# Hybrid decoder layer with a product-key expert mixer: picks of the gathered block paced over all groups, three one-hot groups in ten from ScalarE, up rows three deep, gathers four turns later

## The chip, the cores and the metric

The kernel runs on one core of a Trainium2 chip. Time is device time of one execution in microseconds (us); the number to predict is the median of the runs of the changed kernel. Engines are named as in the profile: PE (TensorE), with PEld for its weight loads, DVE (VectorE), ACT (ScalarE), POOL (GpSimd) and SP (SyncE, which issues most DMAs).

## What is computed

One decoder layer on 512 tokens of width 1024. Its front half (gated DeltaNet heads, pooling groups, output projection) is not touched. The second half is a mixer over 128 x 128 = 16,384 single-neuron experts: for each token and each of 8 heads, 16 experts are found by product keys, and their outputs are added with a softmax gate.

```python
def block(xb):
    q = (xb @ w_query).reshape(t, PEER_HEADS, 2, PEER_HALF)
    scores = jnp.einsum("thpc,hpkc->thpk", q, sk)
    s1, i1 = lax.top_k(scores[:, :, 0], PEER_TOPK)
    s2, i2 = lax.top_k(scores[:, :, 1], PEER_TOPK)
    ...
    top_s, top_pos = lax.top_k(cand, PEER_TOPK)
    idx = jnp.take_along_axis(cand_idx, top_pos, axis=-1)
    gate = jax.nn.softmax(top_s, axis=-1)
    u = expert_down[idx]
    v = expert_up[idx]
    act = jax.nn.gelu(jnp.einsum("td,thkd->thk", xb, u), approximate=False)
    return jnp.einsum("thk,thkd->td", gate * act, v)
```

## The kernel before

The 512 tokens are four blocks of 128. Block 0 is the **gathered** block: its experts' rows are fetched by indirect DMA, one row tile (128 tokens x 1024) for each of its 128 slots, first from `down` and then from `up`. Blocks 1 to 3 (384 tokens) are **dense**: PE computes the hidden value of every expert (128 tiles of 128 experts, "tile" below), multiplies it by a gate matrix that is zero almost everywhere, and multiplies the product by `up`.

After the queries (`query`, `topk`) and the first 17 tiles (`make_ahead`), the second half of the program has three stages.

**The hole before the gates.** PE turns the dense blocks' indices and gates into rows by three groups of transposes, `i1a`, `i2a` and `ex` (the softmax's result). `ex` needs an exponential on ACT and four DVE instructions, and DVE copies the results to `i1t`, `i2t`, `gtt`.

**The gates.** 96 groups of four tokens. For a group DVE builds two one-hot factors: `ob` (position of the second key times the gate, four TENSOR_SCALAR, L850) and `oa` (position of the first key, one TENSOR_TENSOR, L852). PE multiplies them (`g_ps`, L857), ACT copies the result into `stg` (L860), POOL copies part of each full `stg` to `gsb` and SP writes the rest to DRAM (`gmat`). When the group's number mod 10 is in `A_ACT`, DVE makes only `ob` (one TENSOR_TENSOR, L841), and ACT makes `oa` from eight ACTIVATEs (L845, L846). `oa` and `ob` have four buffers each, `g_ps` six, `stg` one.

Between the groups two other things run. `take` spends **steps** of tiles on PE: a step is three matmuls (L126 to L128) and eight steps are a tile. Each tile needs its weights split into `w_hi` on ACT (L616) and `w_lo` on POOL (L617). And `picks` walks through the top-k of the gathered block on DVE in 28 pieces, which end in the indices `eidx` (L809) and the gates `gat`. A scheduler sets the order on each engine from the program order, priorities and modelled times; `issue_after` ties an instruction behind another in that order.

**The turns.** 128 turns of the last loop, one for each tile of experts. A turn loads a row block of `up` (`u_raw`, two buffers), splits it into `u_hi` (ACT) and `u_lo` (DVE, L121), multiplies hidden values and gates (`w`, DVE L957), splits that into `whi` and `wlo`, and PE adds 18 matmuls to `acc` (L940). Every fourth turn loads a new `gsb`. Most turns also compute one more tile (`refill`), with `w_lo` on DVE. The gathers run beside this: POOL issues a row (L915), DVE multiplies and adds it (L917), with four row buffers; `gather_goal` says how many of the 256 have been taken by the end of a turn. After the loop the outputs are normalised and written.

Of the kernel before, what the change touches and what calls it, by code (L numbers as in the profile page):

```python
# [7 lines left out]
F32 = mybir.dt.float32  # L8
# [10 lines left out]
P = 128  # L19
T = 512  # L20
D = 1024
DC = D // P
# [7 lines left out]
NK = 128  # L30
# [10 lines left out]
FAR = 26  # L41
S_QUERY = 7
S_WAIT = 10
S_FIRST = 16
AHEAD = RUN + FAR
LEAD = 4
FAR_TILES = [RUN + ((2 * k + 1) * (NK - RUN)) // (2 * FAR) for k in range(FAR)]
A_ACT = (2, 7)

C_ID, C_U, C_M0, C_MS, C_IO, C_ONE = 0, 128, 256, 384, 384 + 7 * 128, 384 + 8 * 128  # L50
C_RAT = 384 + 9 * 128
# [21 lines left out]
def hymba_peer_block(ctx, tc, consts, x, nmix, w_in, w_ba, conv_w, a_log, dt_bias, dn_w, w_pool, pool_scale,  # L73
                     w_out, nffn, w_q, sub_k, downT, down, up, nfin, out):
    nc = tc.nc
# [8 lines left out]
    iota = cst[:, C_IO:C_IO + P]  # L84
# [64 lines left out]
    with ExitStack() as fx:  # L149
# [227 lines left out]
        with ExitStack() as f2:  # L377
# [77 lines left out]
            steps = [(lv, tb) for lv in range(1, 7) for tb in range(NTB)]  # L455
# [201 lines left out]
    def ahead_steps():  # L657
        pair = load_pair(downT[ahead[made[0]]], nc.gpsimd)
        while made[0] < AHEAD:
            i, now = ahead[made[0]], pair  # L660
            made[0] += 1
            for k, _ in enumerate(s_steps(i, now)):
                if not k and made[0] < AHEAD:
                    pair = load_pair(downT[ahead[made[0]]], nc.gpsimd)
                yield
# [62 lines left out]
    def softmax(pool, dst, sc, behind=None):  # L728
        n = sc.shape[1]
        nc.vector.tensor_sub(dst, sc, sc[:, :, 0:1].broadcast_to([P, n, K]))  # L730
        with tc.issue_after(behind.ins) if behind is not None else ExitStack():
            nc.scalar.activation(dst, dst, AF.Exp)
        sm = pool.tile([P, n], F32, name="sm", bufs=1)
        nc.vector.tensor_reduce(sm, dst, axis=AX.X, op=ALU.add)
        nc.vector.reciprocal(sm, sm)
        nc.vector.tensor_tensor(dst, dst, sm[:, :, None].broadcast_to([P, n, K]), op=ALU.mult)

    with ExitStack() as fy:
        tk = fy.enter_context(tc.tile_pool(name="tk", bufs=2))
        p_pj = fy.enter_context(tc.tile_pool(name="p_pj2", bufs=2, space=PSUM))  # L740
        p_sc = fy.enter_context(tc.tile_pool(name="p_sc", bufs=4, space=PSUM))
        skt = tk.tile([P, 16, NK], F32, name="skt", bufs=1)
        nc.scalar.dma_start(out=skt, in_=sub_k)
        SA = [P, NDT, PH, K]
        i1a = tk.tile(SA, F32, name="i1a", bufs=1)
        i2a = tk.tile(SA, F32, name="i2a", bufs=1)
        tsa = tk.tile(SA, F32, name="tsa", bufs=1)

        def query(h, eng):
            qh = tk.tile([P, 2, T], F32, name="qh")  # L750
            w = [load_pair(w_q[2 * h + p], eng) for p in range(2)]
            ps = [p_pj.tile([P, 512], F32, name="q_ps") for p in range(2)]
            parts = [slice(0, T)] if h else [slice(0, T // 2), slice(T // 2, T)]
            for ts in parts:
                for p in range(2):
                    for c in range(DC):
                        mm3(ps[p][:, ts], (w[p][0][:, c, :], w[p][1][:, c, :]), (xn_hi[:, c, ts], xn_lo[:, c, ts]),
                            c == 0, c == DC - 1)
            for p in range(2):
                cp = nc.scalar.copy(qh[:, p], ps[p])  # L760
            behind[:] = [None, cp.ins]
            sc = tk.tile([P, NDT, 2, NK], F32, name="sc")
            ps = [p_sc.tile([P, 512], F32, name="sc_ps") for _ in range(NTB)]
            for p in range(2):
                for tb in range(NTB):
                    nc.tensor.matmul(ps[tb][:, p * NK:(p + 1) * NK], qh[:, p, tb * P:(tb + 1) * P],
                                     skt[:, 2 * h + p, :], start=(p == 0), stop=(p == 1))
            for tb in range(NTB):
                nc.scalar.copy(sc0[:, tb, h] if tb < NG else sc[:, tb - NG],
                               ps[tb][:, :2 * NK].rearrange("p (a k) -> p a k", a=2))  # L770
            return sc

        sc = query(0, nc.vector)
        for h in range(PH):
            sc_next = query(h + 1, nc.gpsimd) if h + 1 < PH else None
            for _ in topk(tk, sc, NDT, tsa[:, :, h, :], i1a[:, :, h, :], i2a[:, :, h, :]):
                pass
            sc = sc_next
            if sc is not None:
                make_ahead(h + 1)  # L780
        make_ahead(S_QUERY + S_WAIT)
        ex = tk.tile(SA, F32, name="ex", bufs=1)
        softmax(tk, ex.rearrange("p b h k -> p (b h) k"), tsa.rearrange("p b h k -> p (b h) k"), s_act[0])
        for src, dst in ((i1a, i1t), (i2a, i2t), (ex, gtt)):
            ps = p_pj.tile([P, 512], F32, name="q_ps")
            with tc.issue_after(s_last[0].ins):
                for b in range(NDT):
                    pe_last = nc.tensor.transpose(ps[:, b * P:(b + 1) * P], src[:, b].rearrange("p h k -> p (h k)"),
                                                  ident)
            nc.vector.tensor_copy(dst, ps[:, :TD])  # L790
            if dst is not i2t:
                nc.scalar.activation(n1t if dst is i1t else ngt, ps[:, :TD], AF.Copy, scale=-1.0)
# [3 lines left out]
    with ExitStack() as fy:  # L796
# [17 lines left out]
        gs = fy.enter_context(tc.tile_pool(name="gs", bufs=3))  # L814
        p_g = fy.enter_context(tc.tile_pool(name="p_g", bufs=6, space=PSUM))
        gsb0 = gp.tile([P, NTG, GN * TG], F32, name="gsb")

        steps = ahead_steps()
        taken = 0

        def take(goal):
            nonlocal taken, pe_last
            while taken < goal:
                with tc.issue_after(pe_last.ins):
                    next(steps, None)
                pe_last = s_last[0]
                taken += 1

        n_steps = (AHEAD - S_QUERY - S_WAIT) * DC
        take(S_FIRST)  # L830
        ng = 0
        for tg in range(NTG):
            stg = gs.tile([P, NK, TG], F32, name="stg", bufs=1)
            for q in range(TG // 4):
                oa = gs.tile([P, 4, P], F32, name="oa", bufs=4)
                ob = gs.tile([P, 4, P], F32, name="ob", bufs=4)
                ps = p_g.tile([P, 512], F32, name="g_ps")
                t0 = tg * TG + q * 4
                q4 = [P, 4, P]
                if ng % 10 in A_ACT:  # L840
                    nc.vector.tensor_tensor(ob, iota[:, None, :].broadcast_to(q4),  # L841
                                            i2t[:, t0:t0 + 4, None].broadcast_to(q4), op=ALU.is_equal)
                    for u in range(4):
                        t = t0 + u
                        nc.scalar.activation(oa[:, u], iota, AF.Abs, bias=n1t[:, t:t + 1])  # L845
                        nc.scalar.activation(oa[:, u], oa[:, u], AF.Relu, scale=ngt[:, t:t + 1], bias=gtt[:, t:t + 1])  # L846
                else:
                    for u in range(4):
                        t = t0 + u
                        nc.vector.tensor_scalar(ob[:, u], iota, i2t[:, t:t + 1], gtt[:, t:t + 1], op0=ALU.is_equal,  # L850
                                                op1=ALU.mult)
                    nc.vector.tensor_tensor(oa, iota[:, None, :].broadcast_to(q4),  # L852
                                            i1t[:, t0:t0 + 4, None].broadcast_to(q4), op=ALU.is_equal)
                ng += 1
                with tc.issue_after(pe_last.ins):
                    for u in range(4):
                        pe_last = nc.tensor.matmul(ps[:, u * P:(u + 1) * P], ob[:, u], oa[:, u], start=(u == 0),  # L857
                                                   stop=(u == 3))
                take(S_FIRST + ng * (n_steps - S_FIRST) // (TD // 4))
                nc.scalar.copy(stg[:, :, q * 4:q * 4 + 4], ps.rearrange("p (t i) -> p i t", i=NK))  # L860
                if ng * n_picks // (TD // 4) > picked:
                    next(picks)
                    picked += 1
            sv = stg.rearrange("p i t -> p (i t)")
            nc.gpsimd.tensor_copy(gsb0[:, tg, :], sv[:, :GN * TG])
            nc.sync.dma_start(out=gmat[tg, :, GN * TG:], in_=sv[:, GN * TG:])
# [4 lines left out]
    with ExitStack() as fz:  # L871
# [73 lines left out]
        for i in range(NK):  # L945
            if i and i % GN == 0:
                gsb = gp.tile([P, NTG, GN * TG], F32, name="gsb")
                nc.sync.dma_start(out=gsb, in_=gmat[:, :, i * TG:(i + GN) * TG].rearrange("g p x -> p g x"))
            raw = up_p.tile([P, D], F32, name="u_raw")
            nc.sync.dma_start(out=raw, in_=up[i * NK:(i + 1) * NK, :])  # L950
            uhi = up_p.tile([P, D], F32R, name="u_hi")
            ulo = up_p.tile([P, D], F32R, name="u_lo")
# [33 lines left out]


def gather_goal(i, n):
    return min(n, (i + 1) * n // (NK - 4))


_ORDER = ["consts", "x", "nmix", "w_in", "w_ba", "conv_w", "a_log", "dt_bias", "dn_w", "w_pool", "pool_scale",
# [54 lines left out]
```

## Time and profile before

| | us |
|---|---|
| median of 3 runs (1625.0 to 1626.75) | 1625.88 |
| the profiled execution, its own time | 1620.72 |
| span of that execution in the profile | 1619.0 |
| PE busy in the span | 1550.8 |
| DVE busy | 1288.7 |
| ACT busy | 667.8 |
| POOL busy | 598.1 |

The profile shows one execution. Its rows name an instruction by engine, source line, operation and `out<-in`. Busy time of PE comes from matmuls that overlap, so a PE that shows full can still differ in pace; idle time before a row stands in brackets behind it, with what ended it. The second half of the program begins at about 300 us; the hole before the gates lies at 478 us, the gates run until about 723 us, and the turns from 725 us to about 1600 us.

### The profile page before, as it was taken

The numbers are of one execution on the slowest core, as the hardware profiler recorded it, in microseconds if no ns is written. First come the engines' busy times: TensorE is split into PE (matmuls) and PEld (weight loads), VectorE is DVE, ScalarE is ACT, GpSimd is POOL, SyncE is SP. The second block draws the span as 40 slices with busy tenths as digits, with TensorE's granted clock in tenths as the row PEclk, the third lists the DMA queues.
The fourth block names the chain that finished last, engine by engine and source line by source line (L and its number), as shares of the span: only waits on it lengthen the run. The fifth ranks groups of instructions, "written<-read, shape, count | busy, mean of one in ns | idle before, by whom it ended". The sixth has DMA issues, their size and how long they took to land.

```text
span 1619.0 us, 23396 instructions
## 1 busy us (share of the span) xinstructions
PE 1550.8 (96%) x8417; PEld 1394.1 (86%) x8417; DVE 1288.7 (80%) x2666; ACT 667.8 (41%) x1097; POOL 598.1 (37%) x389
## 2 busy tenths in 40 slices
PE   6999999999989878999999999999999999999996
PEld 5888788888989878997788888888888889888885
DVE  5576656799989999986878877777878878778785
ACT  5545343433336546662333333333333333333333
POOL 2003230144453322325544444454434444444331
PEclk9999999999999999999999999999999999999998
DMA  6221121422343444569999998999998999989972
GB/s 207 79 66 54 56 90 40 157 91 92 94 128 126 178 182 175 192 226 377 366 327 325 306 329 308 332 320 321 318 321 308 322 317 329 324 303 338 311 266 76
DMA packets 142388, 367.32 MB, mean 227 GB/s; under 512 B 11232, under 2 KB 65520, under 8 KB 140608
## 3 DMA queue, kind: packets, MB, share of 16 engines
q1 hardware_dynamic: 104272, 227.34, 41.0%
q0 software_dynamic: 37856, 137.44, 23.9%
q8 instruction: 66, 1.08, 0.3%
q10 hardware_dynamic: 144, 1.05, 0.2%
q14 instruction: 50, 0.41, 0.1%
HBM read 331.58 MB, written 34.21 MB: 226 GB/s over the span
## 4 chain that ended last, share of the span: by engine, by line
PE 78%; DVE 13%; DMA 3%; POOL 2%; issue 2%; ACT 2%; SPq 0%; POOLq 0%; ACTq 0%; DVEq 0%
PE acc L940 30%; PE s_ps L126 9%; PE s_ps L128 8%; PE s_ps L127 8%; DVE ob L850 4%; PE pj L126 3%; PE pj L127 3%; PE pj L128 3%; DVE oa L852 2%; PE q_ps L127 2%; PE q_ps L126 2%; PE q_ps L128 2%; PE g_ps L857 2%; DMA row<-in_down_dram,eidx 1%; POOL row L915 1%
## 5 line engine op out<-in xcount | busy, mean ns | idle before, releaser
L126 PE MATMUL s_ps<-xn_hi,w_hi 128*128 128x384 f32 x1024 | 357.7, 349 | 0.0
L128 PE MATMUL s_ps<-xn_hi,w_lo 128*128 128x384 f32 x1024 | 346.9, 339 | 1.6 <-POOL w_lo L617 1.5
L127 PE MATMUL s_ps<-xn_lo,w_hi 128*128 128x384 f32 x1024 | 346.3, 338 | 0.0
L616 ACT ACTIVATE w_hi<-w_raw 128x1024 fp32r<-128x1024 f32 x144 | 152.8, 1061 | 334.8 <-PE s_ps L127 267.3
L924 POOL DMA_INDIRECT row<-in_up_dram,eidx x128 | 189.1, 1477 | 237.0 <-DVE xr L926 208.2
L915 POOL DMA_INDIRECT row<-in_down_dram,eidx x128 | 191.3, 1495 | 215.9 <-DVE row L917 190.3
L617 POOL TENSOR_TENSOR w_lo<-w_raw,w_hi 128x1024 fp32r<-128x1024 f32 x60 | 154.9, 2582 | 284.5 <-ACT w_hi L616 245.0
L940 PE MATMUL acc<-u_lo,whi 128*128 128x512 f32 x768 | 239.0, 391 | 7.3 <-DVE u_lo L121 7.3
L940 PE MATMUL acc<-u_hi,whi 128*128 128x512 f32 x768 | 239.8, 393 | 0.1
L940 PE MATMUL acc<-u_hi,wlo 128*128 128x512 f32 x768 | 238.6, 391 | 0.0
L120 ACT ACTIVATE whi<-w 128x384 fp32r<-128x384 f32 x128 | 67.2, 525 | 321.0 <-issue 268.4
L126 PEld LDWEIGHTS s_ps<-xn_hi,w_hi 128*128 128x128 f32 x1024 | 194.0, 189 | 3.2
L127 PEld LDWEIGHTS s_ps<-xn_lo,w_hi 128*128 128x128 f32 x1024 | 193.9, 189 | 3.2
L128 PEld LDWEIGHTS s_ps<-xn_hi,w_lo 128*128 128x128 f32 x1024 | 193.5, 189 | 2.2 <-POOL w_lo L617 2.2
L121 DVE TENSOR_TENSOR wlo<-w,whi 128x384 fp32r<-128x384 f32 x128 | 71.1, 555 | 143.8 <-ACT whi L120 143.6
L940 PEld LDWEIGHTS acc<-u_lo,whi 128*128 128x128 f32 x768 | 144.7, 189 | 39.9 <-DVE u_lo L121 8.7
L940 PEld LDWEIGHTS acc<-u_hi,wlo 128*128 128x128 f32 x768 | 145.0, 189 | 30.3 <-DVE wlo L121 0.2
L917 DVE SCALAR_TENSOR_TENSOR row<-row,xg 128x1024 f32<-128x1024 f32 x128 | 152.3, 1219 | 23.1 <-DMA row<-in_down_dram,eidx 23.1
L926 DVE SCALAR_TENSOR_TENSOR xr<-row,dots,xr 128x1024 f32<-128x1024 f32 x128 | 164.1, 1282 | 5.5 <-DMA row<-in_up_dram,eidx 3.4
L940 PEld LDWEIGHTS acc<-u_hi,whi 128*128 128x128 f32 x768 | 143.6, 189 | 24.4 <-ACT whi L120 0.4
L121 DVE TENSOR_TENSOR u_lo<-u_raw,u_hi 128x1024 fp32r<-128x1024 f32 x128 | 155.9, 1218 | 1.9 <-ACT u_hi L120 1.8
L120 ACT ACTIVATE u_hi<-u_raw 128x1024 fp32r<-128x1024 f32 x128 | 134.2, 1049 | 8.0 <-DMA u_raw<-in_up_dram 8.0
(301 smaller groups left out, 2449.4 us busy)
## 6 DMA issues: line engine op xcount, KB each, us to landing
u_raw<-in_up_dram SPq DMA_DIRECT2D x128, 512.0 KB, 5.9
w_raw<-in_downT_dram SPq DMA_DIRECT2D x128, 512.0 KB, 5.3
gmat<-stg SPq DMA_DIRECT2D x12, 1984.0 KB, 6.5
gsb<-gmat SPq DMA_DIRECT2D x31, 768.0 KB, 7.3
w_raw<-in_w_in_dram SPq DMA_DIRECT2D x20, 512.0 KB, 3.6
w_raw<-in_w_q_dram SPq DMA_DIRECT2D x16, 512.0 KB, 3.6
hfar<-h_far SPq DMA_DIRECT2D x26, 192.0 KB, 2.3
h_act<-hfar SPq DMA_DIRECT2D x26, 192.0 KB, 6.4
```

Of the source, the lines that this page charges most:

```text
L120: nc.scalar.activation(hi, src, AF.Copy)
L121: nc.vector.tensor_sub(lo, src, hi.bitcast(F32))
L126: nc.tensor.matmul(ps, ahi, bhi, start=first, stop=False)
L127: nc.tensor.matmul(ps, ahi, blo, start=False, stop=False)
L128: return nc.tensor.matmul(ps, alo, bhi, start=False, stop=last)
L616: nc.scalar.activation(hi, raw, AF.Copy)
L617: eng.tensor_sub(lo, raw, hi.bitcast(F32))
L915: nc.gpsimd.indirect_dma_start(out=r, out_offset=None, in_=down, in_offset=bass.IndirectOffsetOnAxis(ap=eidx[b][:, s:s + 1], axis=0))
L917: nc.vector.scalar_tensor_tensor(r, r, 1.0, xg, op0=ALU.mult, op1=ALU.mult, accum_out=dots[:, s:s + 1])
L924: nc.gpsimd.indirect_dma_start(out=r, out_offset=None, in_=up, in_offset=bass.IndirectOffsetOnAxis(ap=eidx[b][:, s:s + 1], axis=0))
L926: nc.vector.scalar_tensor_tensor(xr[b], r, dots[:, s:s + 1], xr[b], op0=ALU.mult, op1=ALU.add)
L940: nc.tensor.matmul(acc[b][n], l[:, bs], r[:, n * 512:(n + 1) * 512], start=(i == 0 and l is whi and r is uhi), stop=(i == NK - 1 and l is ...
```

## The change

Four edits. The picks' pieces are tied, each behind the last one-hot of its group (`issue_after(one.ins)`). `A_ACT` goes from two to three groups in ten: 29 of the 96 groups instead of 19 get `oa` from ACT. `u_raw` gets a third buffer, and `gather_goal` is zero until turn 3 and ends at the same turn as before. And `take` is defined earlier: one tile (eight steps) is taken between the transposes of `i2a` and `ex`; `S_FIRST`, the steps taken ahead of the first group, is 20 with these eight, where it was 16.

```diff
-S_FIRST = 16
+S_FIRST = 20
-A_ACT = (2, 7)
+A_ACT = (1, 4, 7)
...
         for src, dst in ((i1a, i1t), (i2a, i2t), (ex, gtt)):
+            if src is ex:
+                take(DC)
             ps = p_pj.tile([P, 512], F32, name="q_ps")
-            with tc.issue_after(s_last[0].ins):
+            with tc.issue_after(pe_last.ins):
...
-                    nc.vector.tensor_tensor(ob, iota[:, None, :].broadcast_to(q4),
+                    one = nc.vector.tensor_tensor(ob, iota[:, None, :].broadcast_to(q4),
...
-                    nc.vector.tensor_tensor(oa, iota[:, None, :].broadcast_to(q4),
+                    one = nc.vector.tensor_tensor(oa, iota[:, None, :].broadcast_to(q4),
...
                 if ng * n_picks // (TD // 4) > picked:
-                    next(picks)
+                    with tc.issue_after(one.ins):
+                        next(picks)
...
-            raw = up_p.tile([P, D], F32, name="u_raw")
+            raw = up_p.tile([P, D], F32, name="u_raw", bufs=3)
...
-    return min(n, (i + 1) * n // (NK - 4))
+    return max(0, min(n, (i - 3) * n // (NK - 8)))
```

On DVE, right behind the factors of the fourth group of the gates. Names: `ob` and `oa` are one-hot factors, `sc`, `val`, `idx`, `rep` and `cand` belong to the picks. Before:

```order
L852 TENSOR_TENSOR oa<-cst,i1t 128x512
L675 MAX val<-sc_2704 128x8 x2
L676 MAX_INDEX idx<-val,sc_2704 128x8
L678 MATCH_REPLACE rep<-val,sc_2704 128x128
L676 MAX_INDEX idx<-val,sc_2704 128x8
L679 MAX val<-rep 128x8
L675 MAX val<-sc_2704 128x8
L680 MAX_INDEX idx<-val,rep 128x8
L676 MAX_INDEX idx<-val,sc_2704 128x8
L678 MATCH_REPLACE rep<-val,sc_2704 128x128
```

and with the change:

```order
L856 TENSOR_TENSOR oa<-cst,i1t 128x512
L675 MAX val<-sc_2704 128x8
L676 MAX_INDEX idx<-val,sc_2704 128x8
L678 MATCH_REPLACE rep<-val,sc_2704 128x128
L679 MAX val<-rep 128x8
L680 MAX_INDEX idx<-val,rep 128x8
L845 TENSOR_TENSOR ob<-cst,i2t 128x512
L854 TENSOR_SCALAR ob<-cst,i2t,gtt 128x128 x4
L856 TENSOR_TENSOR oa<-cst,i1t 128x512
L854 TENSOR_SCALAR ob<-cst,i2t,gtt 128x128 x4
```

Before, four pieces of the picks stand in a row behind the fourth group's factors; now one piece (five instructions) stands between groups, and the next comes three or four groups later.

On PE, at the transposes ahead of the gates (`q_ps<-cst,...` are transposes, `s_ps` are steps of a tile). Before:

```order
L128 MATMUL s_ps<-xn_hi,w_lo 128x384
L788 MATMUL q_ps<-cst,i1a 128x128 x3
L788 MATMUL q_ps<-cst,i2a 128x128 x3
L788 MATMUL q_ps<-cst,ex 128x128 x3
L126 MATMUL s_ps<-xn_hi,w_hi 128x384
```

and with the change, the end of the 24 matmuls that now stand behind `i2a`:

```order
L127 MATMUL s_ps<-xn_lo,w_hi 128x384
L128 MATMUL s_ps<-xn_hi,w_lo 128x384
L804 MATMUL q_ps<-cst,ex 128x128 x3
L126 MATMUL s_ps<-xn_hi,w_hi 128x384
L127 MATMUL s_ps<-xn_lo,w_hi 128x384
```

Eight steps of a tile have moved from behind the transposes of `ex` to before them.

On DVE, where the gates end and the turns begin (`row,dots` are the gathered rows' products, `w_lo` belongs to a refilled tile). Before, some rows behind the first `w`:

```order
L617 TENSOR_TENSOR w_lo<-w_raw,w_hi 128x1024
L121 TENSOR_TENSOR wlo<-w,whi 128x384
L121 TENSOR_TENSOR u_lo<-u_raw,u_hi 128x1024
L617 TENSOR_TENSOR w_lo<-w_raw,w_hi 128x1024
L917 SCALAR_TENSOR_TENSOR row,dots_7351<-row,xg 128x1024 x2
L121 TENSOR_TENSOR wlo<-w,whi 128x384
L917 SCALAR_TENSOR_TENSOR row,dots_7351<-row,xg 128x1024
L121 TENSOR_TENSOR u_lo<-u_raw,u_hi 128x1024
L917 SCALAR_TENSOR_TENSOR row,dots_7351<-row,xg 128x1024 x2
L957 TENSOR_TENSOR w<-h_act,gsb 128x384
```

and with the change:

```order
L617 TENSOR_TENSOR w_lo<-w_raw,w_hi 128x1024
L121 TENSOR_TENSOR wlo<-w,whi 128x384
L121 TENSOR_TENSOR u_lo<-u_raw,u_hi 128x1024
L617 TENSOR_TENSOR w_lo<-w_raw,w_hi 128x1024
L962 TENSOR_TENSOR w<-h_act,gsb 128x384
L121 TENSOR_TENSOR wlo<-w,whi 128x384
L962 TENSOR_TENSOR w<-h_act,gsb 128x384
L121 TENSOR_TENSOR u_lo<-u_raw,u_hi 128x1024
L922 SCALAR_TENSOR_TENSOR row,dots_7614<-row,xg 128x1024
L617 TENSOR_TENSOR w_lo<-w_raw,w_hi 128x1024
```

Five products of gathered rows stood ahead of the fifth turn's `w`; now that `w`, the sixth turn's, and the fourth turn's `wlo` and `u_lo` stand ahead of the first product. At the seam just before these rows, DVE has also got 16 instructions of the last piece of the picks (L708 to L736, `oh`, `eidx` and `gat` among them) between the last `oa` and the first `w`.

## Rows read from the trace of the kernel before

**Rows 1.** The head of the page.
```profile
span 1619.0 us, 23396 instructions
```

**Rows 2.** Stretches: busy us and count of PE, PEld, DVE, ACT, POOL; granted clock; DMA share; GB/s.
```profile
484.00:642.00 158.00, 138.21 (x898) 131.80 (x898) 157.48 (x503) 92.36 (x192) 49.94 (x24) 0.96 0.45 162
642.00:718.00 76.00, 73.62 (x520) 73.14 (x519) 73.38 (x161) 49.80 (x110) 26.94 (x14) 1.00 0.58 212
726.00:800.00 74.00, 66.72 (x309) 58.07 (x308) 57.37 (x87) 23.24 (x33) 41.04 (x29) 0.95 1.01 374
800.00:1500.00 700.00, 700.00 (x3452) 627.65 (x3451) 556.39 (x688) 248.39 (x340) 313.67 (x211) 1.00 0.92 321
...
760.00:770.00 10.00, 10.00 (x45) 8.80 (x45) 9.52 (x16) 3.24 (x5) 6.22 (x5) 0.86 1.03 416
```

**Rows 3.** PE in order of time: start, us, instruction, [idle before <-releaser].
```profile
478.38 0.49 PE L788 MATMUL q_ps<-cst,i2a 128*128 128x128 f32 x3
483.06 0.88 PE L788 MATMUL q_ps<-cst,ex 128*128 128x128 f32 x3 [4.19 <-DVE ex L736]
```

**Rows 4.** Groups by form, 484 to 724 us: count | busy us, mean ns | idle before, releasers.
```profile
L850 DVE TENSOR_SCALAR ob<-cst,i2t,gtt 128x128 f32<-128x128 f32 x308 | 125.3, 466 | 2.6 <-PE g_ps L857 2.6
```

**Rows 5.** DVE in order of time, at the end of the picks.
```profile
642.08 0.24 DVE L809 SCALAR_TENSOR_TENSOR eidx<-i,i 128x128 int32<-128x128 f32 x1
642.24 3.18 DVE L850 TENSOR_SCALAR ob<-cst,i2t,gtt 128x128 f32<-128x128 f32 x4
...
646.14 1.10 DVE L850 TENSOR_SCALAR ob<-cst,i2t,gtt 128x128 f32<-128x128 f32 x4
647.17 0.68 DVE L852 TENSOR_TENSOR oa<-cst,i1t 128x512 f32<-128x512 f32 x1
```

**Rows 6.** POOL: its weight splits by form, 484 to 724 us.
```profile
L617 POOL TENSOR_TENSOR w_lo<-w_raw,w_hi 128x1024 fp32r<-128x1024 f32 x27 | 72.2, 2675 | 129.0 <-ACT w_hi L616 116.1 <-PE g_ps L857 6.3 <-DVE rep L678 5.9
```

**Rows 7.** POOL in order of time, beside Rows 5.
```profile
642.37 2.44 POOL L617 TENSOR_TENSOR w_lo<-w_raw,w_hi 128x1024 fp32r<-128x1024 f32 x1 [3.18 <-ACT w_hi L616]
```

**Rows 8.** ACT in order of time: one group's factor, and the copy behind it.
```profile
577.26 0.70 ACT L845 ACTIVATE oa<-cst,n1t 128x128 f32<-128x128 f32 x2 [4.12 <-PE g_ps L857]
...
580.00 1.52 ACT L860 COPY stg<-g_ps 128x512 f32<-128x512 f32 x3
```

**Rows 9.** PE: the groups' products by form, 484 to 724 us.
```profile
L857 PE MATMUL g_ps<-oa,ob 128*128 128x128 f32 x768 | 105.5, 281 | 20.7 <-DVE oa L852 18.0 <-DVE fij L710 1.5 <-ACT oa L846 1.1
```

**Rows 10.** DVE in order of time, from the last group to the first turn.
```profile
717.71 0.68 DVE L852 TENSOR_TENSOR oa<-cst,i1t 128x512 f32<-128x512 f32 x1
721.02 1.23 DVE L617 TENSOR_TENSOR w_lo<-w_raw,w_hi 128x1024 fp32r<-128x1024 f32 x1 [2.63 <-ACT w_hi L616]
724.53 1.03 DVE L957 TENSOR_TENSOR w<-h_act,gsb 128x384 f32<-128x384 f32 x2 [2.28 <-POOL gsb L865]
```

**Rows 11.** PE in order of time: last steps, first turn, and the turns' two long waits.
```profile
724.58 0.34 PE L127 MATMUL s_ps<-xn_lo,w_hi 128*128 128x384 f32 x1
...
725.11 0.34 PE L127 MATMUL s_ps<-xn_lo,w_hi 128*128 128x384 f32 x1
...
725.70 0.74 PE L940 MATMUL acc<-u_hi,whi 128*128 128x512 f32 x2
...
758.99 0.95 PE L940 MATMUL acc<-u_lo,whi 128*128 128x512 f32 x2 [3.82 <-DVE u_lo L121]
...
789.09 0.73 PE L940 MATMUL acc<-u_lo,whi 128*128 128x512 f32 x2 [3.45 <-DVE u_lo L121]
```

**Rows 12.** Waits from 720 to 800 us: engine and line, releaser: us, times, longest.
```profile
DVE row L917 <- DMA row<-in_down_dram,eidx: 11.6, 9, 5.1
```

**Rows 13.** The picks' last steps on DVE in order of time: from the index arithmetic to `eidx`.
```profile
624.73 0.17 DVE L708 TENSOR_SCALAR ta<-pos 128x32 uint32<-128x32 uint32 x1
...
627.63 1.23 DVE L718 TENSOR_TENSOR oh<-fij,cst 128x1024 bf16<-128x1024 f32 x1
...
638.96 1.27 DVE L725 TENSOR_REDUCE i<-oh 128x32 f32<-128x512 bf16 x2
```

More of the change, by code (lines that the diff above doesn't have):

```diff
@@ L783, in hymba_peer_block, with take @@
         softmax(tk, ex.rearrange("p b h k -> p (b h) k"), tsa.rearrange("p b h k -> p (b h) k"), s_act[0])
+        steps = ahead_steps()
+        taken = 0
+        pe_last = s_last[0]
+        def take(goal):
+            nonlocal taken, pe_last
+            while taken < goal:
+                with tc.issue_after(pe_last.ins):
+                    next(steps, None)
+                pe_last = s_last[0]
+                taken += 1
         for src, dst in ((i1a, i1t), (i2a, i2t), (ex, gtt)):
+            if src is ex:
+                take(DC)
             ps = p_pj.tile([P, 512], F32, name="q_ps")
-            with tc.issue_after(s_last[0].ins):
+            with tc.issue_after(pe_last.ins):
                 for b in range(NDT):
@@ L816, in hymba_peer_block @@
         gsb0 = gp.tile([P, NTG, GN * TG], F32, name="gsb")
[L818 to L827, printed above, removed]
         n_steps = (AHEAD - S_QUERY - S_WAIT) * DC
```

## The prediction

> **What bounds the kernel now.** I read the page's head first [rows 1], then the stretches [rows 2], because a share over the whole span hides which stage has slack. From 800 to 1500 us PE is busy for 700.00 of 700 us at granted clock 1.00, while DVE has 556 and ACT 248: there nothing but PE's own work counts, and no edit here removes any of it. So time can only come from the stages before 800 us, and only where PE waits. There are three places.
>
> The hole before the gates: PE sits idle for 4.19 us until `ex` is ready [rows 3].
>
> The gates: from 484 to 642 us DVE is busy for 157.48 of 158 us and PE for 138.21 [rows 2]. PE's products waited 20.7 us in all, 18.0 of them for `oa` from DVE [rows 9]. From 642 to 718 us both are full, with 73.62 and 73.38 of 76. The reason is order: all 28 pieces of the picks are done by 642.08 [rows 5], so PE first starves and then works off its backlog, and DVE reaches the last group at 717.71 [rows 10]. DVE's time has two parts. Undisturbed, `ob` takes 1.10 us for a group, 1.03 to the start of `oa` (646.14 to 647.17), but at 642.24 it takes 3.18 [rows 5], exactly while POOL splits a weight for 2.44 us from 642.37 [rows 7]. There are 27 such splits in the stage [rows 6], and the 77 groups' `ob` show 125.3 us where 77 x 1.10 = 84.7 would do [rows 4]: 40.6 us of DVE's stage are stalls against POOL.
>
> The first turns: from 726 to 800 us PE has 66.72 of 74 us [rows 2]. It waits twice for `u_lo`, 3.82 and 3.45 us [rows 11], and behind the first wait the granted clock of a 10 us slice is 0.86 [rows 2]. The two levels are 2.4 and 1.2 GHz, so 28% of that slice ran at the lower one, which cost 1.4 us. DVE's queue shows why: products of gathered rows waited 11.6 us for their DMA [rows 12], with `u_lo` queued behind them, while the DMA share was 1.01 [rows 2].
>
> **The change, part by part.** I follow one event, PE's first matmul of the first turn, now at 725.70 [rows 11]; everything after it is PE work plus the waits of the first turns.
>
> *Ten more groups on ACT.* 29 groups instead of 19. Each takes four `ob` of 1.03 off DVE and leaves one TENSOR_TENSOR in place of another: 10 x 1.03 = **-10.3** on DVE, which is the engine that sets the stage. ACT gets 10 x 2.74 us (577.26 to 580.00, [rows 8]) = 27.4. It was busy for 92.36 + 49.80 = 142.2 of the 234 us from 484 to 718 [rows 2], so 169.6 fits, but its queue is in order: an `oa` can stand behind a copy that waits. PE waited 1.1 us for ACT's `oa` with 19 groups [rows 9]; 29 make that 1.7. Two table loads for the gates' exponential now also fall near the end. I take **+2** for both; bounds -1 and +10.
>
> *Picks paced.* No DVE work goes away. But the last piece, 16 instructions from L708 to `gat`, now stands behind the last `oa`: twelve small ones of some 0.16, one of 1.2, a second of that width that I put at 0.7, two reductions in 1.3 [rows 13], about 5.0 in all. So the last `oa` comes **5.0** sooner, and these 5.0 are queued ahead of the first `w_lo` and `w`. With PE's backlog gone, DVE's waits for PE (2.6 us, [rows 4]) mostly go too: **-2**. The last `oa` ended at 718.3, and the first turn began 7.4 later, because PE still had groups to do. Now it is 5.0 + 1.2 (`w_lo`) + 0.5 (`w`) [rows 10] + 0.5 (`whi`, priced like `w`) = 7.2 later: **-0.2**. PE hides little of this; it has one group's products and some steps of 0.53 us left there, about 3 us, and then waits some 4 us. Together with the ACT groups: -10.3 - 5.0 - 2 - 0.2 = **-17.5**, so the first turn starts at about 708.
>
> *Stalls against POOL.* The splits stay 27, so I leave the 40.6 as it is: **0**. Bounds: with 67 groups of `ob` instead of 77 in their way, 40.6 x 67/77 = 35.3, which is -5.3; if every split costs the full 3.18 - 1.10 = 2.08, 27 x 2.08 = 56.2, which is +15.6.
>
> *Eight steps into the hole.* Three matmuls take 0.53 us (724.58 to 725.11, [rows 11]), so a tile is 4.2 and fits the hole of 4.19. The transposes of `ex` stand behind it on PE; from 478.7 it ends at 482.9, and `ex` came at 483.06, so DVE's start is not moved: **0**. The gain for PE (4.2, and the lower clock after the hole) is hidden, since DVE sets the stage; if DVE were faster it would count. If the tile's `w_lo` were late by one split, DVE would start 2.4 later.
>
> Is PE fast enough? From 483.06 to 725.70 are 242.6 us; without its 20.7 of waits for factors and the 4.2 moved into the hole, 217.7 are left, which ends at 700.8. PE has about 7 us in hand against 708.
>
> *Gathers four turns later, `u_raw` three deep.* The products of rows no longer stand ahead of the fifth turn's `w`, `wlo` and `u_lo` on DVE, and that turn's `u_raw` is loaded before the gates end. POOL's first four gathers are not held back by this, only their use is, so they have landed when DVE comes to them. The two waits and their slow clock, 3.82 + 3.45 + 2 x 1.4 = 10.1, should nearly go; I keep 1: **-9**, bounds 0 and -10. Later the gathers run at 256/120 = 2.13 a turn instead of 2.06. From 800 us on DMA is at 0.92 and PE at 700.00 of 700 [rows 2]: priced 0.
>
> **Sum.** -17.5 + 2 - 9 = -24.5. The profiled execution took 1620.72, so 1596.2 by its own clock; the median of the runs is 5.2 higher, 1625.88, and gives **1601**.
>
> **Rivals.** (a) *The waits of the first turns stay*, because the gathers start into a DMA that is as full as before and DVE's queue blocks the same way four turns on: 1601 + 9 = 1610. For it: a DMA share of 1.01 with the up rows and weights in it. Against: four rows are in flight ahead of use. Chance 0.14.
>
> (b) *Each split costs DVE its full length*, because with picks spread out no split finds DVE long in instructions that do not mind POOL: +15.6, 1617. Rows 5 and 7 show one such meeting, but 40.6 / 27 = 1.5 on average speaks for half-hidden ones. Chance 0.10. The Trainium skill, page SBUF — State Buffer, section "Who interferes with whom", calls the port that VectorE and GpSimd share an exclusive lock: the loser blocks for the whole instruction, and tensor_scalar can take that lock, as can two SBUF inputs. By that rule the time is nearer to this rival; the 2.08 us of rows 5 agree with it.
>
> (c) *PE becomes the bound of the gates*, since stalls fall and ACT keeps up: the first turn at 700.8, 24.9 earlier; with -9 that is 1592. Chance 0.12.
>
> (d) *Slower: ACT becomes the bound of the gates.* Its idle time (234 - 142.2 = 91.8) may be waits in queue order that do not shrink. Then the stage takes 169.6 + 91.8 = 261 instead of 234, +27; less 9 for the turns, 1644. It decides where more than 234 + 9 - 169.6 = 73 us of ACT's idle time stay. Against: most of that idle time is waiting for PE, as the 4.12 in rows 8. Chance 0.06. The Trainium skill, page ScalarE: Activation LUTs, section "Rules for kernel authors", says to use VectorE rather than ScalarE for relu and the like; rows 5 and 8 agree that ACT is dearer (2.74 against 1.03), and by that rule the change gives away time. I hold against it that DVE is the full engine here.
>
> (e) *Nothing moves by more than a measurement tells*: the waits return elsewhere one for one. 1626, chance 0.05. That the edits do not take place is excluded by the order on the engines.
>
> **How the numbers follow.** The forecast has 0.53, (a) 0.14, (b) 0.10, (c) 0.12, (d) 0.06, (e) 0.05. The forecast's own range goes by its bounds, -5.3 and -1 for stalls and ACT one way, +10 for ACT the other. With (a) to (c) the range is 1588 to 1617; (d) and (e), 0.11, and some of the tails lie outside. Faster by over 0.2%, which is about what a measurement of this kernel can tell: 0.89; within it 0.05; slower 0.06.
>
> **What would show it.** Right: PE without the 4.19 us hole; `eidx` only after the last `oa`; the first `acc` near 708; DVE still full to the end of the gates with 25 to 30 splits and `ob` of 3 us among those of 1.1; about 4 us of PE idle before the first turn; no wait for `u_lo` above 2 us from there to 800. Wrong: `g_ps` waiting for ACT's `oa` by over 10 us, `ob` losing far more than 40 us, PE waiting for `u_lo` four turns later, or PE below full after 800 us.

## The result and the profile after

The changed kernel takes **1601.99 us** (median of 4 runs, 1600.72 to 1602.75) against 1625.91 before: 0.9852 of the time, 95% interval 0.9835 to 0.9869, so 23.9 us less. The profiled execution took 1602.75, its span is 1601.0.

Busy time of the engines by stretch, as in [rows 2] (us; then the granted clock, the DMA share, GB/s):

```profile
484.00:642.00 158.00, 146.43 (x1004) 142.93 (x1003) 155.72 (x421) 120.09 (x274) 57.13 (x28) 0.99 0.50 184
642.00:708.00 66.00, 58.61 (x396) 57.97 (x397) 65.30 (x182) 44.79 (x104) 18.89 (x10) 0.95 0.54 195
...
718.00:726.00 8.00, 8.00 (x34) 6.89 (x33) 4.59 (x6) 4.03 (x6) 0.00 (x0) 0.83 0.94 376
726.00:800.00 74.00, 74.00 (x367) 66.42 (x366) 58.45 (x85) 26.43 (x36) 36.37 (x27) 1.00 1.00 376
800.00:1500.00 700.00, 700.00 (x3448) 627.38 (x3447) 564.40 (x697) 247.99 (x339) 323.01 (x218) 1.00 0.93 325
```

From 726 to 800 us PE is now full, where [rows 2] have 66.72 of 74, at a DMA share as high as before. In the gates DVE is nearly as full as it was (155.72 of 158, and 65.30 of 66 towards the end). The first 8 us of the turns, from 718 to 726, run at a granted clock of 0.83, behind the two short waits of PE shown below.

DVE at the seam between the gates and the turns (start, duration, what; the last `oa`, the last picks, the refilled tile's `w_lo`):

```profile
709.14 0.69 DVE L856 TENSOR_TENSOR oa<-cst,i1t 128x512 f32<-128x512 f32 x1
...
714.52 0.28 DVE L825 SCALAR_TENSOR_TENSOR eidx<-i,i 128x128 int32<-128x128 f32 x1
...
715.16 1.22 DVE L617 TENSOR_TENSOR w_lo<-w_raw,w_hi 128x1024 fp32r<-128x1024 f32 x1
```

and PE there, with its idle time in brackets:

```profile
714.70 0.34 PE L127 MATMUL s_ps<-xn_lo,w_hi 128*128 128x384 f32 x1
716.43 0.44 PE L128 MATMUL s_ps<-xn_hi,w_lo 128*128 128x384 f32 x1 [1.40 <-DVE w_lo L617]
717.46 1.22 PE L945 MATMUL acc<-u_hi,whi 128*128 128x512 f32 x2 [0.58 <-ACT whi L120]
```

The picks end behind the last `oa`, as they should. But PE's first `acc` stands at 717.46, 8.2 us earlier than the 725.70 of [rows 11] and not 15.5. The last `acc` ended 18.0 earlier (1605.84 to 1587.81), so the turns gave 9.8. The total came out right while its largest part did not; the experiments say why.

### The profile page after: what moved, and what is told of

Read it like the earlier page. It is cut to its first block, busy times and chain, and to the rows that moved or that the text cites. A ratio compares the mean times of both kernels' runs of the same rounds, so it can differ in the third digit from the quotient of the medians.

```text
span 1601.0 us, 23404 instructions
## 1 busy us (share of the span) xinstructions
PE 1545.1 (97%) x8417; PEld 1393.0 (87%) x8417; DVE 1284.6 (80%) x2626; ACT 692.9 (43%) x1177; POOL 595.2 (37%) x389
## 4 chain that ended last, share of the span: by engine, by line
PE 80%; DVE 16%; DMA 1%; ACT 1%; POOL 1%; issue 1%; SPq 0%; ACTq 0%; DVEq 0%; POOLq 0%
PE acc L945 33%; PE s_ps L126 9%; PE s_ps L128 9%; PE s_ps L127 9%; DVE ob L854 6%; PE pj L126 3%; PE pj L127 3%; PE pj L128 3%; DVE oa L856 2%; PE q_ps L127 2%; PE q_ps L126 2%; PE q_ps L128 2%; PE ups L436 1%; PE p L445 1%; DVE ob L845 1%; PE sc_ps L766 1%
```

## The experiments

The same two lengths are used throughout, both from the traces' first and last instructions: the **gates** from the start of `gtt`'s copy on DVE to the first `acc`, and the **turns** from there to the end of the last `acc`. Medians in us; the ratio is to the kernel before on the same chip, with its 95% interval. Rows without a ratio are the kernel before (1625.9 is the median of its 4 runs) or a single execution.

| kernel | median | ratio | gates | turns |
|---|---|---|---|---|
| before, first profile | 1625.9 | | 241.7 | 880.1 |
| before, second profile | 1624.0 | | 243.9 | 879.9 |
| changed | 1602.0 | 0.9852 (0.9835 to 0.9869) | 232.6 | 870.4 |
| before + turns' edit | 1612.4 | 0.9914 (0.9897 to 0.9930) | 243.7 | 868.8 |
| before + later gathers | 1611.9 | 0.9920 (0.9902 to 0.9937) | 244.1 | 868.8 |
| before + third `u_raw` | 1625.2 | 1.0005 (0.9995 to 1.0014) | 244.2 | 881.2 |
| before + ten groups on ACT | 1616.6 | 0.9946 (0.9929 to 0.9963) | 236.9 | 877.6 |
| before + pacing | 1625.0 | 0.9991 (0.9977 to 1.0005) | 243.1 | 883.7 |
| changed - pacing | 1608.8 | 0.9893 (0.9876 to 0.9909) | 240.7 | 868.8 |
| changed - tile in the hole | 1603.6 | 0.9858 (0.9842 to 0.9875) | 233.1 | 870.4 |
| changed + 9 more groups on ACT | 1589.9 | 0.9785 (0.9769 to 0.9802) | 221.0 | 868.8 |
| changed, `w_lo` on DVE | 1579.2 | 0.9713 (0.9697 to 0.9730) | 215.7 | 866.3 |
| changed, memset for the split | 1573.3 | | 205.5 | 868.8 |
| changed, `w_lo` on DVE, 9 more groups | 1573.9 | 0.9689 (0.9672 to 0.9706) | 205.9 | 868.8 |

**The kernel before once more.**

> The kernel before, profiled once more, since its first profile took 1620.72 where its median is 1626. If the first profile was an ordinary one, gates (gtt on DVE to first acc) of 241.7 and turns (first to last acc) of 880.1 us return within 1 us. If its turns or its gates were lucky, one of the two is 3 to 6 us longer here, and that is the stage to which the difference between the change of medians (-24) and the change of profiles (-18) belongs.

1623.98, with gates of 243.9 and turns of 879.9. With the three runs below that leave the gates' code as it was, there are five profiles of it: 241.7, 243.7, 243.9, 244.1, 244.2. The profile that the prediction read was the shortest, by 2.2 us against the mean of the other four (244.0). The turns of its two profiles agree within 0.3. So the change's gain in the gates is 11.4 against ordinary profiles, 9.1 against that one.

**The turns' edit alone, and each half of it.**

```diff
-    return min(n, (i + 1) * n // (NK - 4))
+    return max(0, min(n, (i - 3) * n // (NK - 8)))
...
-            raw = up_p.tile([P, D], F32, name="u_raw")
+            raw = up_p.tile([P, D], F32, name="u_raw", bufs=3)
```

> The kernel before with the turns' edit alone (gathers' use from turn 4 on, three u_raw buffers). My theory: the gates stage is as before (first acc at 725 to 727 us of the profile) and the two waits for u_lo (3.82 and 3.45 us) with the slow clock behind them go: 9 to 10 us less, 1616 to 1617. Rival, the waits stay or come back four turns on: 1624 to 1626, with a u_lo wait above 2 us before 800 us. Rival, the turns' gain of 9.8 us seen in the changed kernel belongs to the earlier end of the gates: this run gives less than 5.

Both lines: 1612.43, 13.6 less. The gates are those of before, so the whole gain is the edit's own, and more than the 9 that I had priced. The upper line alone:

> The kernel before with the later gathers alone, u_raw two deep. Theory: u_lo was late because the rows' products stood ahead of it on VectorE and waited for their DMA, so this alone gives nearly all of the 11 to 13 us of the two edits: 1612 to 1615. Rival, u_lo was late because u_raw landed late: a u_lo wait stays, 1620 or more.

and the lower alone:

> The kernel before with the third u_raw buffer alone; VectorE's order is that of before. Theory: the rows' products still block the queue, so 0 to 3 us less, 1622 to 1626, and u_lo waits of over 5 us in all stay. Rival, the early load of u_raw is what counts: 1612 to 1616.

The later gathers do all of it, 1611.92 (12.3 less on their chip). The third buffer does nothing that can be measured, 1625.18. Stretch 726 to 800 with the later gathers alone (columns as above):

```profile
726.00:800.00 74.00, 73.92 (x367) 66.17 (x366) 56.45 (x82) 28.20 (x39) 31.62 (x24) 1.00 1.00 374
```

and with the third buffer alone, followed by PE's waits from there on (in total, times, longest):

```profile
726.00:800.00 74.00, 65.73 (x306) 56.57 (x305) 54.70 (x83) 23.19 (x33) 36.83 (x28) 0.95 0.99 367
...
PE acc L940 <- DVE u_lo L121: 8.2, 4, 4.4
```

DVE in the same run, before the fourth turn's `u_lo`:

```profile
744.54 1.23 DVE L917 SCALAR_TENSOR_TENSOR row<-row,xg 128x1024 f32<-128x1024 f32 x1 [5.43 <-DMA row<-in_down_dram,eidx]
...
748.84 1.21 DVE L121 TENSOR_TENSOR u_lo<-u_raw,u_hi 128x1024 fp32r<-128x1024 f32 x1
```

`u_lo` was late because the rows' products stood ahead of it in DVE's queue and waited there for their DMA; with the later gathers it starts at 741.74. It was not late because `u_raw` landed late: with the third buffer the fifth turn's `u_raw` is issued at 309.0 us (736.2 in the second profile of before), and its `u_lo` starts at 760.7 all the same (762.7). The rows also show what I under-priced. The clock of that stretch is 0.95, all of it from two slices of 10 us at 0.83 (760 to 770 and 790 to 800), behind waits. With levels of 2.4 and 1.2 GHz a third of each slice ran at the lower one, which costs 3.4 in all. 8.2 + 3.4 = 11.6, and the turns of the two runs differ by 12.3 (881.15 to 868.83).

**Ten groups to ACT alone.**

```diff
-A_ACT = (2, 7)
+A_ACT = (1, 4, 7)
```

> The kernel before with three groups in ten from ScalarE alone, picks still early. Theory, DVE sets the stage: ten groups fewer of four ob (10 x 1.03) less what ACT's order costs, -8 to -10, first acc near 716, 1616 to 1618. Rival, PE sets the stage once the picks are done (it was busy 73.4 of 76 us from 642 to 718), so that only waits before 642 can go: -2 to -4, 1622 to 1624, with DVE waiting for PE by over 5 us.

9.4 less, of which the gates have 7.1 (244.0 to 236.9) and the turns 2.3, since shorter waits for `u_lo` (6.2 us) at a better clock (0.98 from 726 to 800) happened to follow. Between the theories in the gates: the picks are done at 624.6 and then PE is the full engine.

```profile
642.00:708.00 66.00, 66.00 (x470) 65.91 (x469) 61.80 (x126) 55.22 (x128) 23.30 (x14) 1.00 0.61 223
```

PE has 66.00 of 66, DVE 61.80, with 4.0 us of waits for PE in the gates: about 3 of the 10 us that these groups give beside the pacing (below) are lost here.

**The pacing, taken out of the changed kernel, and alone.**

```diff
                 if ng * n_picks // (TD // 4) > picked:
-                    with tc.issue_after(one.ins):
-                        next(picks)
+                    next(picks)
```

> The changed kernel with the picks as early as before (pacing undone). Theory of my forecast: pacing took 7 us (last piece of 5.0 behind the last oa, waits of 2 gone), so without it 1608 to 1610. Rival, pacing is worth nothing because the pieces between the groups make DVE's instructions dearer by as much: 1601 to 1603, with picks' busy time on DVE some 5 us lower than the 58 us of the changed kernel. Rival, pacing costs: below 1600.

1608.77, so in the changed kernel pacing is worth 6.8 us, in the gates 8.1. Without it the picture of the last run repeats, more strongly. Stretch 642 to 708:

```profile
642.00:708.00 66.00, 65.29 (x461) 64.90 (x461) 58.59 (x123) 53.74 (x123) 22.92 (x12) 1.00 0.58 211
```

and DVE's waits for PE in the gates:

```profile
DVE ob L854 <- PE g_ps L861: 6.7, 11, 1.2
...
DVE ob L845 <- PE g_ps L861: 2.0, 1, 2.0
```

With the pacing one wait of 0.2 us is left of these. Why this kernel's gates are 3.9 longer than with ACT's groups alone, though it has a tile less to do in them, is open: all I see is 4.4 us more of idle time on DVE and picks that end at 638.6 and not 624.6.

The kernel before with the pacing and nothing else:

> The kernel before with the picks' pacing alone (two groups in ten from ScalarE, no tile in the hole, gathers as before). Theory of my forecast, the parts add: the last piece of 5.0 goes behind the last oa and VectorE's waits of 2 to 3 us go, 7 less, 1617 to 1618, gates near 237. Rival, pacing only pays where VectorE would else wait for PE (9 us of waits in the changed kernel with early picks, 3 in the kernel before), and the pieces between the groups cost VectorE 5 us more: 0 to -3, 1622 to 1625, gates 241 to 244.

1625.04: nothing. The gates are 243.1, 0.9 shorter, and the turns 883.7, 3.8 longer: PE waits 9.2 us for `u_lo` (7.6 in the second profile of before), and behind a wait of 2.5 us for `whi` at the seam the granted clock is 0.79 from 726 to 734. So the rival holds, and the parts don't add. With two groups in ten on ACT, DVE is the full engine of the gates. It gains little from an even order, since it hardly waits for PE (2.7 us), while the pieces between the groups cost it more. From `gtt` to the last factor, summed from start to start of its instructions, DVE took 235.9 in the second profile of before and 235.3 here. The picks in that time went from 49.8 (255 instructions) to 52.1, although the last piece (14 instructions, 5 us) had left it; the factors from 182.1 to 177.6; idle time from 3.3 to 4.8.

**The tile in the hole, taken out.**

```diff
-            if src is ex:
-                take(DC)
...
-S_FIRST = 20
+S_FIRST = 16
```

> The changed kernel without the tile in the hole before ex (and 16 steps ahead of the first group, as before). Theory: the hole is hidden since DVE sets the stage: 1601 to 1603, PE idle for about 4 us ahead of ex, gtt on DVE about 0.9 earlier. Rival, PE sets the stage's end in the changed kernel: the 4.2 us of PE work and the slow clock behind the hole come back, 1605 to 1607.

1603.64, and the two intervals nearly coincide: no difference that can be told. The hole is back, 4.2 us of PE idle before `ex`, and the stage keeps its place and length (`gtt` at 485.11 and 484.85, gates 233.1 and 232.6). That is in part a balance: without the tile DVE waits 5.4 us for PE in the gates, where the changed kernel has 0.2, but its stalls, counted as below, are 44.5 and not 48.8. So this run doesn't show that the tile is worth nothing by itself.

**What sets the gates: POOL's split.** In the changed kernel two timelines side by side show the cost. DVE:

```profile
560.20 2.28 DVE L845 TENSOR_TENSOR ob<-cst,i2t 128x512 f32<-128x512 f32 x1
562.40 0.28 DVE L679 MAX8 val<-rep 128x8 f32<-128x128 f32 x1
...
563.00 1.11 DVE L854 TENSOR_SCALAR ob<-cst,i2t,gtt 128x128 f32<-128x128 f32 x4
...
564.62 3.36 DVE L854 TENSOR_SCALAR ob<-cst,i2t,gtt 128x128 f32<-128x128 f32 x4
...
568.50 0.68 DVE L845 TENSOR_TENSOR ob<-cst,i2t 128x512 f32<-128x512 f32 x1
```

and POOL in the same time:

```profile
559.54 2.39 POOL L617 TENSOR_TENSOR w_lo<-w_raw,w_hi 128x1024 fp32r<-128x1024 f32 x1 [9.47 <-ACT w_hi L616]
565.15 2.44 POOL L617 TENSOR_TENSOR w_lo<-w_raw,w_hi 128x1024 fp32r<-128x1024 f32 x1 [3.22 <-ACT w_hi L616]
```

The same `ob` takes 2.28 us during a split and 0.68 without, four TENSOR_SCALAR 3.36 and 1.11. Going through all 28 splits from 480 to 709 us, each but one lengthens exactly one DVE instruction, by 0.5 to 2.24 us, 1.81 on average, 48.8 us together. The victims are mostly `ob`, but also a TENSOR_TENSOR and three instructions of the picks. Counted the same way, the first profile of before has 46.9 (25 events, 27 splits) and the second 49.0: the 40.6 of [rows 4] were those of L850 alone.

To test it, the same split on DVE, for all tiles between the groups but the first:

```diff
             for k, _ in enumerate(s_steps(i, now)):
                 if not k and made[0] < AHEAD:
-                    pair = load_pair(downT[ahead[made[0]]], nc.gpsimd)
+                    pair = load_pair(downT[ahead[made[0]]], nc.vector)
```

> The changed kernel with w_lo of the tiles made between the gates' groups split on VectorE instead of GpSimd. Theory: GpSimd's 27 splits cost VectorE 49 us of stalls; on VectorE itself they cost 27 x 1.22 = 33, so its stage is 16 us shorter, ob falls back to about 0.27 us each, and the time is 1584 to 1590 (PE's 19 us of idle time in the stage is the most that can go). Rival, the long factors have another cause (the order of picks and factors): the move adds 33 us of work to the full engine, 1630 to 1636. Rival, VectorE waits in its queue for w_hi of ACT: in between, with DVE gaps of over 10 us.

1579.21, 22.8 us less than the changed kernel and below the range expected: giving the full engine 31 us of work more made it faster. The gates have 16.9 of it. The turns are 4.1 shorter, because 16 matmuls of refilled tiles (2.5 us) come before the first `acc`, and because the slow clock behind the seam (1.6) is gone. The costliest DVE groups of the gates (count, busy us, mean ns, idle before), changed kernel first:

```profile
L854 DVE TENSOR_SCALAR ob<-cst,i2t,gtt 128x128 f32<-128x128 f32 x268 | 117.2, 489 | 0.3 <-PE g_ps L861 0.2
...
L845 DVE TENSOR_TENSOR ob<-cst,i2t 128x512 f32<-128x512 f32 x29 | 21.4, 737 | 0.0
```

then with the split on DVE:

```profile
L854 DVE TENSOR_SCALAR ob<-cst,i2t,gtt 128x128 f32<-128x128 f32 x268 | 78.5, 336 | 1.4 <-PE g_ps L861 1.3
...
L617 DVE TENSOR_TENSOR w_lo<-w_raw,w_hi 128x1024 fp32r<-128x1024 f32 x29 | 35.3, 1216 | 1.6 <-ACT w_hi L616 1.4
L845 DVE TENSOR_TENSOR ob<-cst,i2t 128x512 f32<-128x512 f32 x29 | 19.7, 680 | 0.1
```

`ob` alone loses 38.7 + 1.7 us of busy time. From `gtt` to the last factor, summed from start to start, DVE's stage goes from 224.3 to 204.4: +30.7 for 27 splits (1.14 each), -40.7 for `ob` by TENSOR_SCALAR, -1.5 by TENSOR_TENSOR, -9.4 for the picks, +1.1 of idle time. By this sum the stalls were 51.6 us, a little more than the 48.8 of the events, and a split cost DVE 1.9 us on POOL where it costs 1.14 on DVE itself.

And with no split at all (the kernel leaves the low half of these weights out):

```diff
-        eng.tensor_sub(lo, raw, hi.bitcast(F32))
+        if eng is None:
+            nc.gpsimd.memset(lo.bitcast(F32), 0.0)
+        else:
+            eng.tensor_sub(lo, raw, hi.bitcast(F32))
...
-                    pair = load_pair(downT[ahead[made[0]]], nc.gpsimd)
+                    pair = load_pair(downT[ahead[made[0]]], None)
```

> The changed kernel with GpSimd's split of the tiles made between the gates' groups replaced by a memset of w_lo to zero, which leaves the low half of those weights out. Theory: without the split no stalls, VectorE's stage 49 us shorter, so PE sets it: 19 to 21 us less, 1581 to 1584, and VectorE waits for PE. Rival, any GpSimd writing into SBUF stalls VectorE as much: 1598 to 1602. Rival, VectorE was not what set the stage: less than 5 us.

1573.28, with PE as the full engine of the gates and DVE waiting for it (10.6 us in the gates; PE, PEld, DVE, ACT, POOL busy):

```profile
484.00:642.00 158.00, 157.13 (x1110) 156.94 (x1109) 147.82 (x480) 131.46 (x302) 24.70 (x31) 1.00 0.57 200
```

That is PE's floor: gates of 205.5. The gain, 28.7, is past the 21 expected, because PE runs at clock 1.00 throughout and waits for 0.9 us only.

**More groups on ACT.**

```diff
-A_ACT = (1, 4, 7)
+A_ACT = (1, 3, 6, 8)
```

> The changed kernel with four groups in ten from ScalarE (38 groups, 9 more). Theory, VectorE still sets the stage and ten groups were worth 8.6 us of its time: 6 to 8 less, 1594 to 1596, ACT's idle time before the end still above 20 us. Rival (d) of the prediction, ACT becomes the bound: PE's g_ps wait for oa of ACT by over 10 us and the time is 1604 or more.

1589.92, 12.1 less for nine groups, more than I expected. DVE's factors are 9.8 shorter, close to 9 x 1.03. The rest comes from the picks, 3.6 shorter against 1.8 more of idle time: one split falls on them where three did, and the stalls together are 43.8, not 48.8. ACT follows; PE's waits in the gates:

```profile
PE g_ps L861 <- DVE oa L856: 4.5, 1, 4.5
PE g_ps L861 <- ACT oa L850: 2.7, 5, 1.0
```

**Both.** Two edits together, `w_lo` on DVE and `A_ACT = (1, 3, 6, 8)`:

> The changed kernel with both: w_lo of the tiles between the gates' groups split on VectorE, and four groups in ten from ScalarE. Theory: with the stalls gone the gates are close to what PE needs, so the two gains (-22.8 and -12.1 alone) don't add to 1567: PE sets the stage as in the run with the memset, 1571 to 1575, VectorE waits for PE by over 5 us. Rival, ACT becomes late (38 groups and 27 w_hi on which VectorE now waits): 1579 or more, with g_ps waiting for ACT's oa.

1573.93, 28 us faster than the changed kernel and 3.1% faster than the one before (0.9689, 0.9672 to 0.9706).

```profile
484.00:642.00 158.00, 157.38 (x1108) 156.72 (x1107) 153.59 (x469) 148.61 (x359) 5.96 (x9) 1.00 0.56 204
642.00:680.00 38.00, 38.00 (x273) 38.00 (x272) 37.30 (x123) 36.99 (x92) 1.27 (x2) 1.00 0.67 233
```

PE is full in the gates too, and their 205.9 us match those of the memset run. The two gains (22.8 and 12.1) don't add, since the floor lies 28 below. The theory was right in size and wrong in a detail: DVE waits for PE only 2.5 us, so DVE (153.59), ACT (148.61) and PE are all near full here.

## Why the prediction was right, and where it was wrong

The forecast of 1601 missed by 1 us. That is partly luck: by the medians of the runs, the gates' term was too large by about 5 (10.4 for 15.5), and the turns' too small by as much (13.6 for 9).

*The reading of the bounds* held. DVE sets the gates: a shorter stage on DVE gave 12.1 and 22.8 us in runs where PE's work stayed the same. PE's own work sets the turns: in the six kernels of the table where PE has no wait and no slow clock behind the first `acc`, and the same matmuls, they take 868.8.

*Ten groups to ACT*, -10.3 + 2: right where the picks are paced. Pacing alone has gates of 243.1, pacing and the ten groups 233.1 (the kernel without the hole's tile): 10.0. The +2 for ACT was hardly needed: PE waited 2.9 us for ACT's `oa` (1.1 in [rows 9]), and the time from the last `oa` to the first `acc` is 8.3 (8.0 before). By themselves the groups give 7.1, because PE is next.

*Picks paced*, -7.2 with the seam: this is the step that failed. From `gtt` to the last factor DVE took 233.7 us in the profile that I read and 224.3 in the changed kernel, 9.4 less and not 17.3: the factors 8.6 less (forecast 10.3), the idle time 0.8 (2), the picks nothing (5.0), although the last piece has left that time. Two premises were wrong. First, "no DVE work goes away" left out that time is added. The 252 instructions of the picks up to the softmax's sum, summed from start to start, take 52.6 us early and close together in the profile that I read and 49.3 in the second one. 6.6 and 3.2 of these are stalls, so about 46 is the time undisturbed. In pieces between the factors with no splits beside them (`w_lo` on DVE) they take 48.2, and in the changed kernel 57.6, of which 6.5 are stalls: 2 us more for being in pieces, and 3 more beside the splits that I can't place. Second, DVE's waits for PE, which pacing removes, were 2.6 us before, but 4.0 with the ten groups alone and 8.7 in the changed kernel without the pacing. Pacing is no term of its own: in the gates it gives 0.9 alone and 8.1 beside the ten groups.

*Stalls*, 0: by events +1.9 in all against the first profile of before, -0.2 against the second. The factors have 42.3 of them, where they had 40.4 and 45.8 with ten groups more of `ob` in the way. The price of rival (b) was nearly right, since most events are near the 2.08 read from [rows 5], but the splits cost that much before too. So the change is none here, and my lower bound (-5.3) did not come: a split nearly always finds some DVE instruction to lengthen. The sum is not fixed by the number of splits, though: it is 43.8 with nine groups more on ACT, and 44.5 without the hole's tile.

Together the gates were forecast 15.5 shorter (first `acc`), and measured 8.2 against the profile that I read, 11.5 against ordinary ones, and 10.4 between the medians of the kernel with the turns' edit alone and the changed one. About 5 too much.

*The hole*, 0: right in the time, within 1.7 us; the run behind it balances waits against stalls.

*First turns*, -9: the mechanism was right and the size too small. By the turns' length the edit gives 11.1 to 12.4 (868.8, where the two profiles of before and that of the third buffer have 880.1, 879.9 and 881.2), by medians 12.3 and 13.6. The slow clock costs 3.4 from 726 to 800 in the profile that I read too, not 2.8; and keeping 1 us of waits was not needed, as none are left. In the changed kernel itself the turns are 870.4 and the gain 9.7, since the slow clock at their start takes 1.6 back; the prediction had seen idle time at the seam and given its clock no price. The second reason given, the early `u_raw`, is refuted.

*The basis.* On the profiled execution's own clock the forecast was 1596.2, and the profile of after took 1602.75. Adding the 5.2 by which the first profile lay below its median made the total fit. That is fair in kind, since that profile was a quick draw of the gates by 2.2 and of `gtt`'s start by 1.0 (483.97, in the other four 484.97), but no reading of the profile had said so. Between the second profile of before and that of the changed kernel lie 21.2, not 23.9.

*Rivals.* (a) fell: no `u_lo` wait after the change. (c) fell, and its floor was far off: PE could have begun the turns at 689.6 (the memset run), not 700.8. Taking PE's waits off its time in the gates forgot the time it spends at the lower clock behind them: 0.96 over 158 us in [rows 2] is 6.3 us of the difference; the rest stays open. (d) fell with nine groups more. The Trainium skill, page ScalarE: Activation LUTs, section "Rules for kernel authors", keeps relu on VectorE; in this kernel moving 10 and 9 groups the other way took 9.4 and 12.1 us off, because VectorE was the full engine. (e) holds for single edits (pacing, third buffer, hole) and not for the whole.

*What would show it*: the missing hole, `eidx` behind the last `oa`, DVE full with 28 splits and `ob` of 3 us, no `u_lo` wait came as said; the first `acc` at 708 (710 with the prediction's own +2 for ACT) and 4 us of PE idle before it did not (717.46, and 1.40 + 0.58), because PE's last steps cover the picks' last piece.

## What to carry to other kernels

When one engine stalls another, count the stalls by the instructions that cause them first, and only then by those that suffer. Here moving ten groups of victims away saved nothing and nine more about 5 us, while moving the cause to the stalled engine paid although that engine was full (1.14 us of work for 1.8 to 1.9 us of stall). An edit that evens out the order is worth what the engine then waits for its neighbour: price it together with the edits that change who is next, not as a term of a sum. And read a second profile of the kernel before where its one profile lies 0.3% off the median, since the quick stage may be the one that you price.

## What the runs showed of the hardware

A memset on POOL, which reads no SBUF, disturbs DVE as well, though less: of 27 memsets of 0.97 us, 12 lengthened a TENSOR_SCALAR `ob`, by 0.3 to 0.7 us, and one a TENSOR_SCALAR of the picks by 0.3 (by how much later the next instruction starts). TENSOR_TENSOR `ob` were not lengthened by it (0.69 us on average, 0.77 at most), while a split took one of them to 2.28. MAX8 and FIND_INDEX8 run through a split untouched (0.27 to 0.30 us beside one), so a split that starts among picks costs less (0.5 us at 573.91). The Trainium skill, page SBUF — State Buffer, section "Who interferes with whom", says that the second to issue blocks until the first is done, and that an instruction with two SBUF inputs contends with a GpSimd instruction that reads SBUF but not with one that only writes; both agree with these numbers (the four `ob` from 564.62 end at 567.98, just behind the split that ends at 567.59).

Short waits on PE cost a quarter to a half as much again through the clock, by the turns of three runs: 8.2 us of waits came with a loss of 3.4 us at a granted clock of 0.95 from 726 to 800 (third buffer), 7.3 with 3.4 at 0.95 (before, first profile), and 6.2 with 1.7 at 0.98 (ten groups on ACT).
